# PSUM pools opened from both ends, and one gate's projection moved in among the index scores

## The chip, the core and the metric

The kernel runs on one core of a Trainium2 chip. The metric is the device time of one execution in microseconds (us); lower is better. Five engines matter: TensorE (PE, with its weight loads shown apart as PEld), VectorE (DVE), ScalarE (ACT), GpSimd (POOL) and SyncE (SP), which issues most of the transfers. Each engine works through a list of its own, in order.

## The reference, cut to what matters

The reference is a two-layer encoder on 1024 tokens of width 1024. Layer 0 projects the input once and feeds two groups of heads. Group A is RWKV-7 time mixing (8 heads of 64). Group B is sparse attention: a small indexer scores all admissible keys for each query, the largest 256 scores are kept, and attention runs over these alone. Each group is multiplied by a gate path of its own:

```
score = sum over h of wi[q,h] * relu(qi[q,h] . ki[s])      # the index scores
keep  = the top 256 scores of each query
gate  = silu(x @ W_gate)                                   # 512 columns for A, 512 for B
out   = concat(A * gate_A, B * gate_B) @ W_out
```

Layer 1 is gated linear attention with a gate path and an output projection. After each layer comes h = LayerNorm(alpha * h + sublayer(h)).

## The kernel before

Every projection works on numbers split into a high and a low part, so a product takes three matmuls for each of the eight blocks of the inner dimension. `mm_fm` (L215 to L223) makes 128 output columns for 512 tokens in 24 matmuls, `mm_cols` two such halves for all 1024 tokens, into a two-bank PSUM tile `dn`. `wcols` loads the 128 weight columns (`craw`), casts them to a high part on POOL (`chi`, L231) and makes the low part there (`clo`, in the helper at L103). `craw` has one buffer, `chi` and `clo` have three each.

The stages around the change, in order:

1. The index stage. The loop over `ORD` runs index scores by query tile (0 to 7), queries of the attention (10 and 11), a weight load (9) and keys and values (8). `index_scores` is matmuls L447 into `dn` or `ix`, a relu on ACT (L453) into `rl`, and a multiply-add on DVE (L458) into `sc`.
2. The projection stage, for j from 0 to 3. First comes the rank projection (`rank_inputs`, with a tanh at L686). Then, per j, the three token-shifted projections of group A (`shifted`, with the ACT and DVE steps L549 and L550 into `sh`, which has three buffers), the operands of the recurrence (`operands`, L615 to L634, with POOL multiplies in the helper at L103), and the gates listed in `PG`. `gate(z)` is 48 matmuls, a tanh on ACT (L539), a multiply-add on DVE (L540) and a store `d_gate`. All of this is interleaved with the top-256 selection: counting passes on DVE (L741 to L748) and passes of signs on ACT (L771 to L773), one after the other for each tile.
3. Sparse attention (logits at L925) and RWKV, whose order is pinned; then the output projection of layer 0, layer 1, its gates and its output projection. `gate_piece` (matmuls L243 to L245 into bank `gt`, tanh L1624, multiply-add L1625) is the last gate work; `l1_half` then transposes (L1704) the gated values, casts them (`yh` L1706, `yl` L1707) and multiplies them with the output weights (L868). The last four weight blocks arrive in `wraw` and become `whi` and `wlo` (L182, L183).

A list scheduler fixes each engine's order when the program is built: it takes the instructions in program order as priorities and places each where its plan says its inputs are ready. An engine can't depart from that order on the chip.

PSUM has eight banks. `open_psum` closes the old pool and opens a new one at each stage; a pool is a region, and the first tile of a new pool waits for all of the older pool whose region it takes. The stages use these banks: ps0 (index and projections) `tr` 2, `dn` 2 tiles of two banks, `ix` 2; ps1 (attention and RWKV) `s`, `po`, `g`, `x`, `ca`, `cb`; ps2 `dn`, `tr`; ps3 (layer 1) `att`, `dn`, `tr`, `gt` 2; ps4 (last output projection) `tr` 3, `op` 3.

Of the kernel before, what the change touches and what calls it, by code (L numbers as in the profile page):

```python
# [8 lines left out]
F32 = mybir.dt.float32  # L9
# [4 lines left out]
AF = mybir.ActivationFunctionType  # L14
ALU = mybir.AluOpType
# [3 lines left out]
PSUM = bass.MemoryType.PSUM  # L19
DRAM = bass.MemoryType.DRAM  # L20

P = 128
SEQ = 1024
NT = 8
# [27 lines left out]
SB = 3  # L52
# [15 lines left out]
LG = 7  # L68
QA = (2, 3)
OG = (0, 0, 0, 0, 0, 0, 3, 2, 3, 0, 0)  # L70
ORD = (2, 3, 4, 9, 10, 5, 7, 11, 6, 8)
PG = [[], [0, 1], [], [], [2, 3], [4], [5], [6, 7], [], []]
RK1 = 0

C_R, C_K, C_V, C_WA = 0, 512, 1024, 1536
C_GA, C_QB, C_IX, C_GB = 1664, 2176, 2688, 3112
# [8 lines left out]
def trunk(ctx: ExitStack, tc: tile.TileContext, x, positions, e_w_in, a_mu, a_w0, a_w2, a_a0, a_a2,  # L85
          a_kk_scale, a_ka, a_rk, a_gn_g, a_gn_b, b_kv_norm_g, b_wuk, b_wuv, e_w_out, o_w_in, c_g2,
          c_g_bias, c_norm_g, o_w_out, ln_g, ln_b, out, dbg=None, stop=None):
    nc = tc.nc
    V, A, G, PE = nc.vector, nc.scalar, nc.gpsimd, nc.tensor
# [15 lines left out]
    def gsub(out, a, b):  # L105
        cut(G.tensor_sub, out, a, b)
# [19 lines left out]
    ewi, ewo, owi, owo = e_w_in[0], e_w_out[0], o_w_in[0], o_w_out[0]  # L126
# [10 lines left out]

    psum = {}

    def open_psum(name, dn, **bank):  # L140
        if psum:
            psum["ctx"].close()
        es = ExitStack()
        ctx.callback(es.close)
        psum.update(ctx=es, pool=es.enter_context(tc.tile_pool(name=name, bufs=1, space=PSUM)), dn=dn, bank=bank)

    def dtile():
        return psum["pool"].tile([P, 1024], F32, name="dn", tag="dn", bufs=psum["dn"])

    def ptile(tag, bufs=None):  # L150
        return psum["pool"].tile([P, 512], F32, name=tag, tag=tag, bufs=psum["bank"].get(tag, 1))

    open_psum("ps0", 2, tr=2, ix=2)

    def rsqrt(pool, xin, n, tag):

# [56 lines left out]
    def wblock(wr, w, c0, n, **kw):  # L213
        return [wload(wr, w, c0, n, k, **kw) for k in range(NK)]

    def mm_fm(pst, wb, cs, ah, al, half):

        sl = slice(half * 512, half * 512 + 512)
        for k in range(NK):
            wh, wl = wb[k]  # L220
            PE.matmul(pst, wh[:, cs], ah[:, k, sl], start=(k == 0), stop=False)  # L221
            PE.matmul(pst, wh[:, cs], al[:, k, sl], start=False, stop=False)  # L222
            PE.matmul(pst, wl[:, cs], ah[:, k, sl], start=False, stop=(k == NK - 1))  # L223

    def wcols(pool, w, c0):

        raw = pool.tile([P, NK, P], F32, name="craw", tag="craw", bufs=1)
        nc.sync.dma_start(raw, w[:, c0:c0 + P].rearrange("(k p) c -> p k c", p=P))
        hi = pool.tile([P, NK, P], F32R, name="chi", tag="chi", bufs=3)
        lo = pool.tile([P, NK, P], F32R, name="clo", tag="clo", bufs=3)  # L230
        CPY[0](hi, raw)  # L231
        gsub(lo, raw, f32(hi))
        return [(hi[:, k], lo[:, k]) for k in range(NK)]
# [31 lines left out]
    d_gate = dram.tile([8, P, SEQ], F32, name="d_gate")  # L265
# [6 lines left out]
    def scope():  # L272
        es = ExitStack()
        ctx.callback(es.close)
        return es
# [7 lines left out]
    wr_ctx = scope()  # L283
    wr = wr_ctx.enter_context(tc.tile_pool(name="wr", bufs=1, side="right"))

    xh = big.tile([P, NK, SEQ], F32R, name="xh")
    xl = big.tile([P, NK, SEQ], F32R, name="xl")
# [58 lines left out]
    gt = gt_ctx.enter_context(tc.tile_pool(name="gt", bufs=1))  # L346
# [50 lines left out]
    for t in range(NT):  # L397
        pt = dtile()
# [12 lines left out]
    for t0 in (0, 4):  # L411
        pt = ptile("tr")
# [22 lines left out]
    def index_scores(i):  # L435
        n = P * (i + 1)
        acc = sc[:, soff[i]:soff[i] + n]
        qiT = index_queries(i)
        E = G if i in IXG else V
        for h in range(8):  # L440
            pt = None
            wide = h in IXW
            if wide:
                pt = dtile()
            for a, b in banks(n):
                ps = pt[:, a:b] if wide else ptile("ix")[:, :b - a]
                PE.matmul(ps, qiT[:, h, :], kiT[:, a:b], start=True, stop=True)  # L447
                if wide:
                    if b < n:
                        continue  # L450
                    a, ps = 0, pt[:, :n]
                r = ixp.tile([P, SEQ], F32, name="rl", tag="rl", bufs=2)[:, :b - a]
                A.activation(r, ps, AF.Relu)  # L453
                w = wi_s[:, i, h:h + 1]
                if h == 0:
                    E.tensor_scalar(acc[:, a:b], r, w, None, op0=ALU.mult)
                else:
                    E.scalar_tensor_tensor(acc[:, a:b], r, w, acc[:, a:b], op0=ALU.mult, op1=ALU.add)  # L458
        V.memset(acc[0:CH, n - CH:n], FMIN)

    def keys_values():
        V.tensor_scalar(ssq, ssq, 1.0 / P, RMS_EPS, op0=ALU.mult, op1=ALU.add)
        rs8 = rsqrt(cp, ssq, NT, "rsq8")
        ktm = t1.tile([P, NT, CH], F32, name="ktm")
        for t0 in (0, 4):
            pk = ptile("ix")
            for t in range(t0, t0 + 4):
                cn = t1.tile([P, P], F32, name="cn", tag="cn", bufs=2)
                V.tensor_scalar(cn, ixt[:, t, 0:P], rs8[:, t:t + 1], None, op0=ALU.mult)
                pt = ptile("tr")  # L470
                PE.transpose(pt[:, :P], cn, ident)
                cT = t1.tile([P, P], F32, name="cT", tag="cT", bufs=2)
                A.activation(cT, pt[:, :P], AF.Copy, scale=par[:, KVG:KVG + 1])
                PE.matmul(pk[:, (t - t0) * P:(t - t0 + 1) * P], cT, wkv, start=True, stop=True)
            pk3 = pk.rearrange("p (t q) -> p t q", q=P)
            A.copy(ktm[:, t0:t0 + 4, :], pk3[:, :, 0:CH])
            A.copy(v_tm[:, t0:t0 + 4, :], pk3[:, :, CH:])
        rope(ktm.rearrange("p t (h d) -> p t h d", h=1), NT, 1, 8, 0, 1)
        k4 = [t1.tile([P, SEQ], F32R, name=f"k4{z}", tag="sp4", bufs=2).rearrange("p (t a d) -> p t a d", a=2, d=CH)
              for z in range(2)]  # L480
        kb = ktm[:, :, None, :].to_broadcast([P, NT, 2, CH])
        A.copy(k4[0], kb)
        V.tensor_sub(k4[1], kb, f32(k4[0]))
        for z, dst in ((0, KH2), (1, KL)):
            for t0 in (0, 4):
                pt = ptile("tr")
                for t in range(t0, t0 + 4):
                    PE.transpose(pt[:, (t - t0) * P:(t - t0 + 1) * P], f32(k4[z][:, t].rearrange("p a d -> p (a d)")), ident)
                A.copy(dst[:, t0 * P:(t0 + 4) * P], pt)

    def queries(t0, wb):
# [6 lines left out]
        for t in range(4):  # L498
# [9 lines left out]
                A.copy(qT[:, h0:h0 + 4, :], pt.rearrange("p (h q) -> p h q", q=P))  # L508
            nc.sync.dma_start(d_q[t0 + t], f32(qT))

    for z in ORD:
        if z < NT:
            index_scores(z)
        elif z == 8:
            keys_values()
        elif z == 9:
            wb = wblock(wr, ewi, C_QB, 512)
        else:
            queries(4 * (z - 10), wb)
# [3 lines left out]
    t1_ctx.close()  # L523
    if stop == "idx":
        return
    wr_ctx.close()
    wr_ctx = scope()
    wr = wr_ctx.enter_context(tc.tile_pool(name="wc", bufs=1, side="right"))

    def proj(c0):  # L530
        pt = dtile()
        mm_cols(pt, wcols(wr, ewi, c0), xh, xl)
        return pt

    def gate(z):
        g, j = divmod(z, 4)
        pt = proj((C_GB if g else C_GA) + j * P)
        o = st("sh", bufs=3) if z >= LG else gt.tile([P, SEQ], F32, name="sg")
        A.activation(o, pt, AF.Tanh, scale=0.5)  # L539
        V.scalar_tensor_tensor(o, o, 1.0, pt, op0=ALU.add, op1=ALU.mult)  # L540
        nc.sync.dma_start(d_gate[z], o)
# [157 lines left out]
    for j in range(3):  # L699
        rank_weights(j)  # L700
        for z in PG[2 * j]:
            gate(z)
# [3 lines left out]
        for h in range(2):  # L706
            kk = operands(j, h, r, k, rn, decays(j, h, t2), t2)
            bonus(j, h, v, kk, brk)
            tokens(j, h, v)
        for z in PG[2 * j + 1]:  # L710
            gate(z)
# [101 lines left out]
    for i in SELO:  # L813
        n = P * (i + 1)
        xs = sc[:, rng(i)]
        z = col[i]
# [13 lines left out]
    j = 3  # L830
    rank_weights(j)
    for z in PG[6]:
        gate(z)
# [3 lines left out]
    rn = norms(j, k)  # L837
    for z in PG[8]:
        gate(z)
    dec = [decays(j, 0, t2), decays(j, 1, t3)]  # L840
    for z in PG[9]:
        gate(z)
# [4 lines left out]
    for h in range(2):  # L847
        bonus(j, h, v, kks[h], brk)
    for z in PG[7]:
        gate(z)  # L850
# [35 lines left out]


    inorder = (tc.keep_in_program_order if PIN_ else (lambda ins: ins))
    open_psum("ps1", 0, s=SB)
    at_ctx = scope()  # L890

    qp = ctx.enter_context(tc.tile_pool(name="qp", bufs=1, side="right"))
# [627 lines left out]


    open_psum("ps2", 3, tr=2)
    g_ctx = scope()
    gp = g_ctx.enter_context(tc.tile_pool(name="gp", bufs=1, side="right"))
# [21 lines left out]
    pt = dtile()  # L1546
# [16 lines left out]
    for h in range(4):  # L1563
        pt = dtile()
# [27 lines left out]
    for z, (c0, dst, ex) in enumerate(((O_Q, qg, la), (O_K, kg, eb))):  # L1592
        wb = wpairs(owi, c0)
        for j in range(4):
            pt = dtile()
# [3 lines left out]
    l_ctx.close()  # L1599


    open_psum("ps3", 2, tr=1, gt=2)
    ga_ctx = scope()
    ga = ga_ctx.enter_context(tc.tile_pool(name="ga", bufs=1, side="right"))
    cngh = ga.tile([P, 2], F32, name="cngh")
# [27 lines left out]
    for t in range(NT):  # L1633
# [6 lines left out]
        po = dtile()  # L1640
        for h in range(4):
            o = po[:, h * 256:(h + 1) * 256]
# [106 lines left out]
```

## Time and profile before

| | |
|---|---|
| Median of 3 runs | 1256.58 us (1253.75 to 1260.7) |
| The profiled execution | 1257.07 us, of which the span is 1255.3 us |
| Instructions in the trace | 22100 |
| Granted TensorE clock, mean share of full speed | 0.977 |
| Longest chain: PE, DVE, DMA | 54%, 15%, 9% of the span |

The span runs from the first to the last recorded instruction; the execution's own time is 1.77 us longer. The chain is followed back from the last instruction, at each step to what released it, so its shares say which engine set the end, not which was busy.

### The profile page before, as it was taken

Reading aid. Unit: us, or ns where it says so; the run is one execution under the profiler, and the core shown is the slowest. Engines: PE = TensorE matmul, PEld = TensorE weight load, DVE = VectorE, ACT = ScalarE, POOL = GpSimd, SP = SyncE. Lnnn points to the kernel's source line nnn. Section 1 sums busy time; section 2 is a strip of 40 time slices with the busy share of each in tenths; the row PEclk is TensorE's granted clock in tenths of the full one; section 3 lists DMA queues with packets and bytes.
Section 4 is the critical chain, followed back from the end, with each engine's and each line's share of the span. In section 5 each row is a group of like instructions: output and inputs, shape, how many; then the busy total and the mean of one; then the engine's idle time right before and its main releaser. Section 6 shows DMA issues by size and latency. Waiting matters only on the chain.

```text
span 1255.3 us, 22100 instructions
## 1 busy us (share of the span) xinstructions
PE 1165.0 (93%) x8125; PEld 934.3 (74%) x8125; DVE 764.7 (61%) x1795; ACT 640.5 (51%) x1395; POOL 409.2 (33%) x723
## 2 busy tenths in 40 slices
PE   7998799989999877989888999999999999998997
PEld 6986587767677666777776777787788788886885
DVE  5145869999985866687776544982601134534666
ACT  5247859889878465666675321324811034413010
POOL 3233853545453034355454300603033120221000
PEclk9999899999999978999998999999999999999999
DMA  6102312544434584444454555842022010014221
GB/s 217 39 5 84 101 51 60 155 101 136 120 101 118 170 222 126 118 117 111 115 148 119 149 169 186 271 159 74 1 68 67 7 62 1 29 40 143 76 101 51
DMA packets 166095, 131.40 MB, mean 105 GB/s; under 512 B 61684, under 2 KB 139556, under 8 KB 165988
## 3 DMA queue, kind: packets, MB, share of 16 engines
q1 hardware_dynamic: 162864, 122.46, 33.5%
q10 hardware_dynamic: 3124, 7.54, 1.9%
q8 instruction: 64, 1.05, 0.3%
q14 instruction: 43, 0.35, 0.1%
HBM read 86.44 MB, written 42.99 MB: 103 GB/s over the span
## 4 chain that ended last, share of the span: by engine, by line
PE 54%; DVE 15%; DMA 9%; issue 8%; ACT 7%; POOL 4%; SPq 2%; DVEq 0%; ACTq 0%; POOLq 0%
PE op L868 7%; PE s L868 5%; DVE fe L741 4%; PE dn L221 4%; PE dn L222 4%; PE dn L223 4%; PE gt L245 2%; PE gt L244 2%; PE gt L243 2%; DMA wraw<-in_e_w_in_dram 2%; PE s L954 1%; PE tr L244 1%; PE tr L243 1%; PE tr L245 1%; PE po L988 1%
## 5 line engine op out<-in xcount | busy, mean ns | idle before, releaser
L103 POOL TENSOR_TENSOR w<-qT,w 128x256 fp32r<-128x256 f32 x104 | 77.7, 782 | 208.0 <-ACT w L203 198.8
L221 PE MATMUL dn<-xh,chi 128*128 128x512 f32 x336 | 135.3, 403 | 5.5 <-DVE sh L550 4.9
L223 PE MATMUL dn<-xh,clo 128*128 128x512 f32 x336 | 133.9, 399 | 0.0
L222 PE MATMUL dn<-xl,chi 128*128 128x512 f32 x336 | 133.3, 397 | 0.0
L203 ACT CAST w<-qT 128x512 fp32r<-128x512 f32 x64 | 38.9, 620 | 105.2 <-PE dn L223 68.1
L741 DVE TENSOR_SCALAR_CACHE_REDUCE fe<-sc,F 128x512 bf16<-128x512 f32 (+2 forms) x93 | 81.6, 877 | 2.5
L221 PEld LDWEIGHTS dn<-xh,chi 128*128 128x128 f32 x336 | 64.0, 190 | 23.1 <-DVE sh L550 6.6
L222 PEld LDWEIGHTS dn<-xl,chi 128*128 128x128 f32 x336 | 63.9, 190 | 15.8 <-issue 2.9
L223 PEld LDWEIGHTS dn<-xh,clo 128*128 128x128 f32 x336 | 63.8, 190 | 14.0 <-issue 1.0
L103 POOL TENSOR_TENSOR clo<-craw,chi 128x256 fp32r<-128x256 f32 x84 | 69.9, 862 | 0.8
L868 PE MATMUL op<-w,yh 128*128 128x512 f32 x192 | 60.4, 399 | 1.7 <-ACT yh L1706 1.7
L458 DVE SCALAR_TENSOR_TENSOR sc<-rl,wi_s,sc 128x384 f32<-128x384 f32 (+5 forms) x42 | 45.1, 1075 | 23.7 <-ACT rl L453 21.2
L935 ACT ACTIVATE w<-w,am 128x128 f32<-128x128 f32 (+7 forms) x64 | 49.6, 775 | 18.8 <-DVE am L933 17.7
L954 PE MATMUL s<-ident,w 128*128 128x128 f32 x288 | 48.9, 296 | 8.9 <-ACT w L935 4.0
L927 DVE CUSTOM_DVE_ANT_0 w<-s,bias_s 128x512 f32<-128x512 f32 (+1 forms) x80 | 45.3, 592 | 18.5 <-PE s L926 18.1
L103 POOL TENSOR_TENSOR vg<-vg,sg 128x256 f32<-128x256 f32 x32 | 24.1, 775 | 99.5 <-DVE vg L1671 53.7
L956 ACT COPY pT<-s 128x512 f32<-128x512 f32 x72 | 42.0, 585 | 20.0 <-PE s L954 19.1
L243 PE MATMUL gt<-w,hh 128*128 128x512 f32 x128 | 51.9, 406 | 0.0
L245 PE MATMUL gt<-w,hl 128*128 128x512 f32 x128 | 51.2, 400 | 0.0
L244 PE MATMUL gt<-w,hh 128*128 128x512 f32 x128 | 51.1, 399 | 0.0
L221 PE MATMUL dn<-hh,w 128*128 128x512 f32 x128 | 50.6, 395 | 0.0
L222 PE MATMUL dn<-hl,w 128*128 128x512 f32 x128 | 50.6, 395 | 0.0
(478 smaller groups left out, 3327.7 us busy)
## 6 DMA issues: line engine op xcount, KB each, us to landing
qT<-in_o_w_in_dram SPq DMA_DIRECT2D x48, 256.0 KB
craw<-in_e_w_in_dram SPq DMA_DIRECT2D x21, 512.0 KB
xt<-in_x_dram SPq DMA_DIRECT2D x8, 512.0 KB
d_q<-qiT SPq DMA_DIRECT2D x8, 512.0 KB
d_ar<-ar SPq DMA_DIRECT2D x8, 512.0 KB
AT<-d_ar SPq DMA_DIRECT2D x32, 128.0 KB
BK<-d_bk SPq DMA_DIRECT2D x8, 512.0 KB
BD<-d_bd SPq DMA_DIRECT2D x8, 512.0 KB
```

The source lines that it names most:

```text
L103: return [f(out[:, a:min(n, a + w)], *(z[:, a:min(n, a + w)] for z in ins)) for a in range(0, n, w)]
L221: PE.matmul(pst, wh[:, cs], ah[:, k, sl], start=(k == 0), stop=False)
L222: PE.matmul(pst, wh[:, cs], al[:, k, sl], start=False, stop=False)
L223: PE.matmul(pst, wl[:, cs], ah[:, k, sl], start=False, stop=(k == NK - 1))
L243: PE.matmul(pst, ah[:, k, sl], wh, start=(k == 0), stop=False)
L244: PE.matmul(pst, ah[:, k, sl], wl, start=False, stop=False)
L245: PE.matmul(pst, al[:, k, sl], wh, start=False, stop=(k == NK - 1))
L741: V.tensor_scalar(junk[:, :P * (i + 1)], sc[:, rng(i)], Ff[:, z] if b < 31 else 0.0, None, op0=ALU.is_ge, op1=ALU.add, accum_out=cnt[:, z])
L868: ins = PE.matmul(pt, a[:, k, :], b, start=(k == 0 and z == 0), stop=(k == NK - 1 and z == 2))
L927: V.tensor_tensor_reduce(ps[h][:, a:b], pt, bias[:, a:b], 1.0, -3e38, op0=ALU.add, op1=ALU.max, accum_out=mx[:, h, z:z + 1])
L935: A.activation(ps[k][:, :n], ps[k][:, :n], AF.Exp, scale=0.125, bias=m[:, k:k + 1], accum_out=rsum[:, k:k + 1])
L954: inorder(PE.transpose(pt[:, j * P:(j + 1) * P], OUT[i]["ps"][2 * j + s][:, kt * P:(kt + 1) * P], ident))
```

## The change

`open_psum` may now open two pools: the tags named in `other` get a pool that is laid out from the other end of PSUM. ps0 puts `tr` and `ix` there, ps1 `s` and `po`, ps3 `gt`; ps2 and ps4 stay single. Each of the two pools is a region of its own, so a tile of the next stage waits for the one it takes.

Gate 0 is taken out of the projection stage (`PG[1]` loses it) and put into the `ORD` loop between the index scores of tile 7 with the queries of the upper half, and those of tile 6. It is done by `gate_halves`: the same weights and the same 48 matmuls, but in two halves of one `ix` bank each, with a tanh and a multiply-add of 512 columns for each half in place of one of 1024. The pool of projection weights (`wc`) is opened there (step 12) and no longer after the loop.

```
-ORD = (2, 3, 4, 9, 10, 5, 7, 11, 6, 8)
-PG = [[], [0, 1], [], [], [2, 3], [4], [5], [6, 7], [], []]
+ORD = (2, 3, 4, 9, 10, 5, 7, 11, 12, 20, 6, 8)
+PG = [[], [1], [], [], [2, 3], [4], [5], [6, 7], [], []]
...
-    def open_psum(name, dn, **bank):
+    def open_psum(name, dn, other=(), **bank):
...
+        pool = es.enter_context(tc.tile_pool(name=name, bufs=1, space=PSUM))
+        high = es.enter_context(tc.tile_pool(name=name + "h", bufs=1, space=PSUM, side="right")) if other else pool
+        psum.update(ctx=es, pool=pool, high=high, other=other, dn=dn, bank=bank)
...
-        return psum["pool"].tile([P, 512], F32, name=tag, tag=tag, bufs=psum["bank"].get(tag, 1))
+        return psum["high" if tag in psum["other"] else "pool"].tile([P, 512], F32, name=tag, tag=tag, bufs=psum["bank"].get(tag, 1))
...
-    open_psum("ps0", 2, tr=2, ix=2)
+    open_psum("ps0", 2, ("tr", "ix"), tr=2, ix=2)
...
+    def gate_halves(z):
+        g, j = divmod(z, 4)
+        wb_ = wcols(wr, ewi, (C_GB if g else C_GA) + j * P)
+        o = gt.tile([P, SEQ], F32, name="sg")
+        for half in range(2):
+            pt, oh = ptile("ix"), o[:, half * 512:half * 512 + 512]
+            mm_fm(pt, wb_, slice(0, P), xh, xl, half)
+            A.activation(oh, pt, AF.Tanh, scale=0.5)
+            V.scalar_tensor_tensor(oh, oh, 1.0, pt, op0=ALU.add, op1=ALU.mult)
+        nc.sync.dma_start(d_gate[z], o)
+
     for z in ORD:
-        if z < NT:
+        if z >= 20:
+            gate_halves(z - 20)
+        elif z == 12:
+            wr_ctx.close()
+            wr_ctx = scope()
+            wr = wr_ctx.enter_context(tc.tile_pool(name="wc", bufs=1, side="right"))
+        elif z < NT:
...
-    wr_ctx.close()
-    wr_ctx = scope()
-    wr = wr_ctx.enter_context(tc.tile_pool(name="wc", bufs=1, side="right"))
...
-    open_psum("ps1", 0, s=SB)
+    open_psum("ps1", 0, ("s", "po"), s=SB)
...
-    open_psum("ps3", 2, tr=1, gt=2)
+    open_psum("ps3", 2, ("gt",), tr=1, gt=2)
```

## Rows read from the trace of the kernel before

**Rows 1.** Page, part 1: busy us, share of span, instructions.

```profile
PE 1165.0 (93%) x8125; PEld 934.3 (74%) x8125; DVE 764.7 (61%) x1795; ACT 640.5 (51%) x1395; POOL 409.2 (33%) x723
```

**Rows 2.** Busy time by stretch: index, then projections.

```profile
core 0: us, PE busy (x) PEld busy (x) DVE busy (x) ACT busy (x) POOL busy (x), PEclk, DMA share, GB/s
131.00:156.47 25.47, 17.80 (x83) 11.90 (x81) 21.98 (x23) 21.42 (x36) 21.08 (x17) 0.92 0.38 125
...
156.00:252.00 96.00, 95.53 (x420) 76.63 (x421) 83.26 (x179) 78.25 (x175) 46.92 (x60) 1.00 0.31 87
252.00:258.00 6.00, 2.10 (x7) 0.82 (x6) 5.96 (x10) 5.18 (x11) 3.36 (x3) 1.00 0.89 219
172.00:398.00 226.00, 218.41 (x907) 168.79 (x905) 195.97 (x393) 201.03 (x483) 108.10 (x136) 0.98 0.42 115
```

**Rows 3.** Timeline of POOL, 118 to 150: start, us, what, idle before.

```profile
129.56 5.68 POOL L103 TENSOR_TENSOR clo<-craw,chi 128x256 fp32r<-128x256 f32 x4
...
144.22 4.75 POOL L103 TENSOR_TENSOR clo<-craw,chi 128x256 fp32r<-128x256 f32 x4
```

**Rows 4.** Timeline of PE at 156 and DVE at 172.

```profile
156.47 0.50 PE L221 MATMUL dn<-xh,chi 128*128 128x512 f32 x1 [0.54 <-ACT rl L453]
...
171.78 0.17 DVE L555 MEMSET bones<- 128x128 f32 x1 [7.77 <-PE tr L488]
```

**Rows 5.** Timeline of ACT, 177 to 180.

```profile
177.48 1.28 ACT L686 ACT_TABLE_LOAD   x1
178.77 1.06 ACT L686 ACTIVATE sh<-sh 64x1024 f32<-64x1024 f32 x1
```

**Rows 6.** Timeline of ACT and DVE at 221: gate 0 as it ran.

```profile
221.31 1.01 ACT L539 ACTIVATE sg<-dn 128x1024 f32<-128x1024 f32 x1
...
222.89 1.22 DVE L540 SCALAR_TENSOR_TENSOR sg<-sg,dn 128x1024 f32<-128x1024 f32 x1
```

**Rows 7.** Timeline of all engines, 251 to 258.

```profile
251.48 2.84 POOL L103 TENSOR_TENSOR kk<-sh 128x256 f32<-128x256 f32 x2 [2.33 <-DVE tha L624]
...
252.30 0.39 PE L223 MATMUL dn<-xh,clo 128*128 128x512 f32 x1
...
254.35 1.11 ACT L549 ACTIVATE sh<-dn,drv 128x1024 f32<-128x1024 f32 x1 [0.54 <-POOL kk L103]
...
257.71 0.50 PE L221 MATMUL dn<-xh,chi 128*128 128x512 f32 x1 [2.21 <-DVE sh L550]
```

**Rows 8.** Timeline of all engines, 436 to 439.

```profile
436.42 0.69 DVE L642 TENSOR_TENSOR kk<-ix,sh 128x512 f32<-128x512 f32 x1
...
437.36 1.15 DVE L540 SCALAR_TENSOR_TENSOR sh<-sh,dn 128x1024 f32<-128x1024 f32 x1
...
438.56 0.33 PE L925 MATMUL s<-KH,qT 128*128 128x128 f32 x1 [3.91 <-DVE sh L540]
```

**Rows 9.** Timeline of all engines, 1143 to 1152: last gate to output projection.

```profile
1143.80 0.72 ACT L206 ACTIVATE w<-qT,cngh 128x512 fp32r<-128x512 f32 x1 [3.20 <-DMA qT<-in_o_w_out_dram]
...
1144.43 0.58 ACT L1624 ACTIVATE sg<-gt 128x512 f32<-128x512 f32 x1
...
1145.22 0.68 DVE L1625 SCALAR_TENSOR_TENSOR sg<-sg,gt 128x512 f32<-128x512 f32 x1
...
1145.96 2.82 PE L1704 MATMUL tr<-ident,vg 128*128 128x128 f32 x12 [3.31 <-DVE sg L1625]
...
1149.04 0.72 ACT L182 ACTIVATE whi<-wraw,cngh 128x512 fp32r<-128x512 f32 x1 [0.59 <-DMA wraw<-in_o_w_out_dram]
...
1149.67 1.54 ACT L1706 CAST yh<-tr 128x512 fp32r<-128x512 f32 x3
...
1150.29 0.73 PE L868 MATMUL op<-w,yh 128*128 128x512 f32 x2 [1.51 <-ACT yh L1706]
```

**Rows 10.** Timeline of DVE and PE, 1165 to 1175.

```profile
1165.47 0.73 DVE L183 SCALAR_TENSOR_TENSOR wlo<-wraw,cngh,whi 128x512 fp32r<-128x512 f32 x1
...
1173.64 1.47 PE L1704 MATMUL tr<-ident,vg 128*128 128x128 f32 x12
```

More of the change, by code (lines that the diff above doesn't have):

```diff
@@ L144, in open_psum @@
         ctx.callback(es.close)
-        psum.update(ctx=es, pool=es.enter_context(tc.tile_pool(name=name, bufs=1, space=PSUM)), dn=dn, bank=bank)
+        pool = es.enter_context(tc.tile_pool(name=name, bufs=1, space=PSUM))
+        high = es.enter_context(tc.tile_pool(name=name + "h", bufs=1, space=PSUM, side="right")) if other else pool
+        psum.update(ctx=es, pool=pool, high=high, other=other, dn=dn, bank=bank)
     def dtile():
```

## The prediction

> **What bounds the kernel now.** I read the page's first part, then the busy times by stretch, then the timeline wherever the diff touches something. The first part makes TensorE look like the bound: 93% of the span, with weight loads at 74% and nothing else above 61% [rows 1]. That average hides stages with different limits, so I read each stage that the change touches.
>
> In the index stage from 131.00 to 156.47 PE works 17.80 us of 25.47 and is idle for 7.67. DVE is idle for 3.49, ACT for 4.05, POOL for 4.39 [rows 2]: nobody is full, the engines take turns. In the projections after it PE looks saturated, 95.53 of 96.00 us up to 252. Then, from 252 to 258, it works 2.10 us of 6.00 while DVE works 5.96 [rows 2]. That hole is the key row of this case. Between the last two gates the product r1 ends its matmuls with the one at 252.30, and the next product starts only at 257.71, released by DVE's L550 [rows 7]. L550 needs L549 on ACT, which at 254.35 was released by POOL's kk, which itself had waited for DVE [rows 7]. So the chain of j=0's operands on DVE, ACT and POOL ends last there, and PE had run ahead of it as far as the three `sh` buffers let it.
>
> **Gate 0 moved: what the index stage pays.** A projection is 48 matmuls; at 95.53 us for 420 instructions one is 0.2275 us [rows 2], so 10.9 us of PE. Its weights' low part is made on POOL at 129.56 to 135.24, in quarters, so the matmuls can begin near 131 [rows 3]. This is the slot of the first weights, which the rank projection uses now; that gets the second, ready at 148.97, and still in time for a start at 156.47 [rows 3, 4]. With PE's 7.67 idle us as cover, 10.9 − 7.67 = 3.2 spill over. Some of PE's 17.80 busy us ran at a granted clock of 0.92 [rows 2]; at full clock they would be 0.08 × 17.80 = 1.4 less, and a spill of 1.8. I take the middle, +2.5.
>
> ACT gets two tanh of 0.58 and the table load of 1.28, DVE two multiply-adds of 0.68 [rows 5, 9]. That is 2.44 and 1.36 against idle times of 4.05 and 3.49 [rows 2]: the idle time hides them; without it they would add their 3.8. So the bounds are 0 (PE's idle fits it and more) and 10.9 + 3.8 = 14.7 (no cover at all). The spill reaches the next stage, because the rank projection starts as PE comes free [rows 4], and DVE's first step of the selection's stage waited 7.77 us for PE [rows 4]. The store of the gate, 128 × 1024 words or 0.52 MB, is now issued by SP in this stretch, where DMA moves 125 GB/s [rows 2]: 4 us of transfer, ahead of SP's later weight loads. Those weights have 156.47 − 148.97 = 7.5 us of slack, so nothing; uncovered it is within the bound above. What POOL does for gate 0 is in the first weights that it prepares now anyway.
>
> **Gate 0 moved: what the projections get back.** PE loses 10.9 us before 252. But PE already waits there for the chain of j=0, so that work is cover for a wait: the hole of about 5 us grows to about 15, and PE's saving is nothing by itself. What the chain itself loses counts: on DVE the multiply-add of 1.22 at 222.89 [rows 6], DVE working 83.26 of 96.00 us there [rows 2]; I take 1.0. On ACT the table load at 177.48, 1.28, and the tanh of 1.01 [rows 5, 6]; ACT works 89% of 172 to 398 (201.03 of 226) and its sign passes follow each other, so part of 2.29: 0.6. Bounds for both together: 0, and the full 10.9 of PE if PE is the limit after all.
>
> The Trainium skill, Perfetto Trace Analysis, section Identifying the Most-Contended Engine, says that matmul busy time is a poor measure of TensorE's headroom because matmuls are pipelined. It wants the share of weight loads instead, and calls the engine of highest occupancy the contended one. In 172 to 398 that is ACT with 89% against 75% of weight loads (168.79 of 226), though the matmuls show 97% [rows 2]. By it, removing matmuls gives nothing here; by the matmul row alone it would give 10.9. The hole at 252 agrees with the page.
>
> The Trainium skill, ScalarE: Activation LUTs, section What ACT_TABLE_LOAD costs, adds a drain of about 1380 ns to each load. The trace does not show one: the ACTIVATE at 178.77 follows the load's 1.28 at once [rows 5]. By the page the index stage would pay 1.4 more and the sum below would be −2.5.
>
> **PSUM of attention.** The first logits at 438.56 waited 3.91 us for DVE's L540, the last gate's reader of `dn` [rows 8]. In the new layout `s` takes the end where `tr` and `ix` were, whose last reader L642 is done at 437.11 [rows 8]. PE could start up to 1.4 earlier, but the attention's first DVE steps still stand behind L540 until 438.51. I take −0.5, between 0 and −1.4. From ps1 to ps2 and ps2 to ps3 nothing changes, as ps2 is one pool over all banks and each of its neighbours waits for all of it.
>
> **PSUM of the last projection.** Here PE stands still. The last gate matmul ends at 1145.96 − 3.31 = 1142.65, and the transposes wait for L1625 on DVE, behind a tanh that sat on ACT behind a weight cast waiting 3.20 us for its transfer [rows 9]. Then the first product waits 1.51 us for `yh` [rows 9]. After the change the transposes' banks were freed long before, by `att`, `dn` and `tr`; only `gt` is read late. They can run at 1142.65, or among the gates. PE's idle there is 3.31 + 1.51 = 4.82, and the twelve transposes took 2.82 us after the stall against 1.47 without one [rows 9, 10]: at most −6.2. The casts stay behind the tanh (ending 1145.01) and two weight casts of 0.72; so the first is done near 1146, and 1150.29 − 1146.0 = −4.3. Lower end: zero, if ACT's order keeps `yh` behind `whi`, which waits for its transfer until 1149.04 [rows 9]; that transfer's buffer is freed by the last gate matmul, which doesn't move. The rest of the weights would not stop it: the last low part is done at 1166.20, and the products that need it run until 1173.64 [rows 10].
>
> **Sum.** +2.5 − 1.0 − 0.6 − 0.5 − 4.3 = −3.9. Against the profiled execution, 1257.07 − 3.9 = 1253.2; that execution is 0.5 above the median of the runs. I predict 1253.0.
>
> **Rivals.**
> - *PE is the bound after all.* The 10.9 us come through, as the new plan lets the matmuls of j=1 and j=2 move up. For it: 97% busy in 172 to 398. Against it: the hole at 252, and a selection that needs no matmul. It replaces −1.6 by −10.9: 2.5 − 10.9 − 0.5 − 4.3 = −13.2, about 1244.
> - *The halves block the index scores* (ends slower). In PE's fixed order 24 matmuls in a row, 5.5 us, stand ahead of the matmuls of tile 6, which ACT and DVE need; they run dry, and the idle is spent waiting for weights instead. Place: 131 to 160. The stage pays 10.9: −3.9 + 8.4 = +4.5, about 1261.6, and up to 1265.4 at 14.7. It decides from a delay of 6.4, where the other terms are used up. For it: PE's waits in this stage are short turns. Against it: nothing makes tile 6 wait except order.
> - *Nothing at the last projection.* ACT's order keeps `yh` behind `whi`. Then the sum is +0.4, about 1257.5. For it: the 1149.04 row. Against it: in a plan, a cast whose input is ready goes ahead of one with a transfer still out.
>
> **How the numbers follow.** Forecast 0.42 (its own range 1249 to 1257), PE the bound 0.28, nothing at the last projection 0.18, index blocked 0.12. What a measurement of this kernel can tell from no change is about 0.5%, 6.3 us: faster is below 1250.3, slower above 1262.9. Faster takes nearly all of the PE rival (0.26) and a tenth from the forecast's low end: 0.36. Slower takes half of the blocked index stage and what its upper end shares with the third rival: 0.09. The rest, 0.55, is the same. The range runs from 1243.5, just below the PE rival, to 1261.6, the blocked stage's own figure; outside lie half of the blocked cases (0.06) and deeper versions of the PE rival (0.1).
>
> **What would show it.** Right: PE busy for nearly all of 131 to 156; a table load there and not at 177; the rank projection starting near 159; a hole in PE of some 15 us where 5 were, before the second product of j=1; the first logits released by L642; the transposes L1704 without a wait for L1625, and the first product near 1146. Wrong: no hole before the product after r1, with the end of the selection some 8 us earlier; a rank projection that starts after 163; or `yh` still behind `whi`.

## The result, and the profile after

The change makes the kernel slower: 1265.61 us median of 19 runs (1260.17 to 1276.83) against 1258.51 of 19 runs before. The ratio is 1.0056, with an interval of 1.0040 to 1.0073. The forecast was 1253.0, and the range ended at 1261.6.

The profiled execution of the change took 1260.9 us, 3.8 more than that of before. Its busy times by stretch, first the index stage as in [rows 2], then the part of it in which most of the gate's matmuls stand, the first products after it, the hole in PE, and the projections:

```profile
core 0: us, PE busy (x) PEld busy (x) DVE busy (x) ACT busy (x) POOL busy (x), PEclk, DMA share, GB/s
131.00:156.47 25.47, 21.81 (x110) 16.87 (x110) 18.16 (x19) 19.15 (x31) 20.45 (x20) 1.00 0.43 145
131.62:147.07 15.45, 15.45 (x76) 12.41 (x76) 9.22 (x9) 11.46 (x16) 12.77 (x13) 1.00 0.38 136
156.00:172.00 16.00, 13.55 (x42) 9.42 (x41) 13.93 (x18) 8.25 (x14) 5.35 (x6) 0.68 0.24 67
252.00:266.00 14.00, 2.21 (x3) 0.67 (x4) 13.82 (x27) 10.36 (x21) 10.66 (x11) 0.61 0.37 105
172.00:398.00 226.00, 209.65 (x880) 162.65 (x879) 194.82 (x391) 193.38 (x463) 109.97 (x131) 0.96 0.38 104
```

In 131.00 to 156.47 PE was busy 4.0 us more (21.81 for 17.80), and from 131.62 to 147.07 without a gap. DVE was busy 3.8 us less (18.16 for 21.98): the scores were pushed out, into 156 to 172. Before, the scores of tile 7 ran from 131.89 to 147.07, and the same columns read for that stretch:

```profile
131.89:147.07 15.18, 9.77 (x45) 6.49 (x44) 11.98 (x9) 12.18 (x18) 15.18 (x12) 0.89 0.46 154
```

There PE was idle for 5.41 us, and POOL for none. PE's and DVE's timelines of the change show how the scores were pushed out (its lines are 3 higher than before for the scores, 16 higher from the projections on):

```profile
131.62 0.50 PE L226 MATMUL ix<-xh,clo 128*128 128x512 f32 x1 [1.03 <-POOL clo L103]
...
134.48 0.63 PE L450 MATMUL dn<-kiT,qiT 128*128 128x512 f32 x2
...
163.82 0.79 PE L224 MATMUL dn<-xh,chi 128*128 128x512 f32 x1 [0.79 <-ACT rl L456]
```

```profile
136.21 1.28 DVE L461 SCALAR_TENSOR_TENSOR sc<-rl,wi_s,sc 128x1024 f32<-128x1024 f32 x1 [2.67 <-ACT rl L456]
...
139.20 1.81 DVE L461 SCALAR_TENSOR_TENSOR sc<-rl,wi_s,sc 128x1024 f32<-128x1024 f32 x1 [1.71 <-ACT rl L456]
...
180.17 0.17 DVE L571 MEMSET bones<- 128x128 f32 x1 [9.83 <-PE tr L491]
```

Between 131.62 and 134.48 twelve gate matmuls run in a row, and only then the score pair of a head of tile 7. The program puts the gate behind tile 7; it is the scheduler's order that has 44 of the 48 matmuls among that tile's scores. ACT's relu and DVE's multiply-add of that head wait, DVE for 2.67 us, and for 1.71 at the next. The rank projection starts at 163.82 where it started at 156.47 [rows 4], and bones comes at 180.17 for 171.78.

At the two ends of the projections, and at the last transition:

```profile
260.97 2.08 PE L656 MATMUL ix<-kk,brk 128*128 128x512 f32 x2 [9.01 <-POOL kk L103]
265.86 0.77 PE L224 MATMUL dn<-xh,chi 128*128 128x512 f32 x1 [2.82 <-DVE sh L566]
```

```profile
1148.16 0.82 PE L1720 MATMUL tr<-ident,vg 128*128 128x128 f32 x6
...
1149.56 0.72 ACT L209 ACTIVATE w<-qT,cngh 128x512 fp32r<-128x512 f32 x1 [3.28 <-DMA qT<-in_o_w_out_dram]
...
1152.14 0.57 ACT L1722 CAST yh<-tr 128x512 fp32r<-128x512 f32 x1
...
1152.76 1.17 PE L884 MATMUL op<-w,yh 128*128 128x512 f32 x2 [3.78 <-ACT yh L1722]
```

The hole in PE has grown, as forecast, though less: to 9.01 + 2.82 = 11.8 us of idle time. Before, it was 2.21 at the product [rows 7] and 1.69 at L640, which is L656 here, so 3.9 in all; the forecast had 5 and 15. The transposes L1720 (L1704 before) no longer wait for the gate [rows 9]; the first product now waits for the cast `yh` instead, 3.78 us.

So that runs can be compared, I read six stretches from each kernel's profiled execution: tile 7 and tile 6 (between the memsets that end a tile's scores; before, these are at 131.89, 147.07 and 161.48), the time from the first score multiply-add (72.2 before) to bones and to RWKV's first instruction (443.74 before), from there to the last gate's tanh (middle), and from that tanh to the last multiply-add with the output product (last). All are us; the ratio is to before, with its interval.

| kernel | tile 7 | tile 6 | bones | RWKV | middle | last | ratio |
|---|---|---|---|---|---|---|---|
| before | 15.2 | 14.4 | 99.6 | 371.5 | 700.7 | 102.0 | |
| the change | 22.6 | 15.1 | 107.5 | 377.9 | 699.6 | 100.0 | 1.0056 (1.0040 to 1.0073) |
| e1 | 15.9 | 13.9 | 100.2 | 374.1 | 705.4 | 101.0 | 1.0005 (0.9981 to 1.0028) |
| e2 | 22.4 | 15.1 | 106.9 | 379.6 | 711.2 | 102.5 | 1.0167 (1.0144 to 1.0190) |
| e3 | 15.2 | 15.8 | 105.5 | 376.9 | 704.5 | 99.9 | 1.0062 (1.0041 to 1.0082) |
| e4 | 15.2 | 14.4 | 99.7 | 377.0 | 700.3 | 102.8 | 1.0011 (0.9985 to 1.0037) |
| e5 | 15.9 | 13.9 | 99.9 | 371.7 | 713.9 | 101.3 | 1.0096 (1.0071 to 1.0120) |
| e6 | 22.3 | 15.1 | 107.1 | 379.7 | 702.8 | 100.6 | 1.0058 (1.0039 to 1.0077) |
| e7 | 15.2 | 14.4 | 93.2 | 367.6 | 716.6 | 102.8 | 1.0089 (1.0070 to 1.0108) |
| e8 | 15.2 | 14.4 | 93.3 | 366.3 | 701.9 | 101.3 | 0.9972 (0.9954 to 0.9991) |
| e9 | 18.3 | 15.5 | 113.5 | 384.8 | 711.4 | 100.3 | 1.0143 (1.0114 to 1.0173) |
| e10 | 15.9 | 13.9 | 93.4 | 367.2 | 703.3 | 101.4 | 0.9979 (0.9958 to 1.0001) |
| e11 | 22.5 | 15.1 | 101.9 | 376.1 | 706.9 | 100.3 | 1.0063 (1.0041 to 1.0085) |
| e12 | 18.5 | 14.7 | 102.1 | 385.2 | 710.8 | 100.4 | 1.0168 (1.0139 to 1.0196) |
| e13 | 18.2 | 17.9 | 105.7 | 376.8 | 701.0 | 101.6 | 1.0043 (1.0017 to 1.0069) |
| e14 | 15.2 | 14.5 | 99.7 | 379.4 | 717.1 | 100.6 | 1.0189 (1.0154 to 1.0224) |

Each stretch is from one execution; where the order of the instructions is the same, tile 7 differs by up to 0.7 us between kernels. Two readings hold over the whole table: "last" is 99.9 to 101.6 with two pools in ps3 and 102.0 to 102.8 with one (before, e2, e4, e7), and "middle" varies by 17 us, though apart from the pools no kernel changes anything in it.

### The profile page after: what moved, and what is told of

Same layout as the page of the kernel before. It is cut to its first block, busy times and chain, and to the rows that moved or that the text cites. A ratio compares the mean times of both kernels' runs of the same rounds, so it can differ in the third digit from the quotient of the medians.

```text
span 1259.2 us, 22105 instructions
## 1 busy us (share of the span) xinstructions
PE 1166.8 (93%) x8125; PEld 935.2 (74%) x8125; DVE 766.0 (61%) x1796; ACT 641.3 (51%) x1396; POOL 409.6 (33%) x723
## 4 chain that ended last, share of the span: by engine, by line
PE 53%; DVE 16%; issue 8%; DMA 8%; ACT 8%; POOL 5%; SPq 1%; DVEq 0%; POOLq 0%; ACTq 0%
PE op L884 7%; PE dn L224 4%; PE dn L225 4%; PE dn L226 4%; PE s L884 3%; DVE fe L757 3%; PE gt L248 2%; PE gt L247 2%; PE gt L246 2%; DMA wraw<-in_e_w_in_dram 1%; PE s L970 1%; ACT fs L787 1%; PE tr L246 1%; PE tr L247 1%; PE tr L248 1%
## 5 line engine op out<-in xcount | busy, mean ns | idle before, releaser
L224 PE MATMUL dn<-xh,chi 128*128 128x512 f32 x320 | 129.9, 406 | 5.1 <-DVE sh L566 4.3
L226 PE MATMUL dn<-xh,clo 128*128 128x512 f32 x320 | 129.0, 403 | 0.0
L225 PE MATMUL dn<-xl,chi 128*128 128x512 f32 x320 | 128.7, 402 | 0.0
L103 POOL TENSOR_TENSOR clo<-craw,chi 128x256 fp32r<-128x256 f32 x84 | 73.2, 900 | 1.0
L951 ACT ACTIVATE w<-w,am 128x128 f32<-128x128 f32 (+7 forms) x64 | 49.5, 774 | 14.5 <-DVE am L949 14.2
L103 POOL TENSOR_TENSOR vg<-vg,sg 128x256 f32<-128x256 f32 x32 | 24.1, 774 | 100.3 <-DVE vg L1687 64.5
L234 POOL CAST chi<-craw 128x1024 fp32r<-128x1024 f32 x21 | 22.2, 1055 | 90.2 <-PE dn L225 56.5
```

Source lines behind the costliest of these rows:

```text
L103: return [f(out[:, a:min(n, a + w)], *(z[:, a:min(n, a + w)] for z in ins)) for a in range(0, n, w)]
L951: A.activation(ps[k][:, :n], ps[k][:, :n], AF.Exp, scale=0.125, bias=m[:, k:k + 1], accum_out=rsum[:, k:k + 1])
```

## The experiments

Theory Q puts the loss in PE's queue in the index stage: the gate's matmuls stand ahead of the score matmuls there, and the delay goes on to the end. Its rivals are the new layout (L), the gate's weights on POOL (W), and the gate's work on ACT and DVE (A). Theories C and B concern what sets the end behind that stage.

**e1: the pools alone.** The two-part `open_psum`, with `ORD` and `PG` of before.

> The PSUM pools in two parts, gate 0 left at j=0. Theory Q (PE's queue: the loss is made in the index stage, where the gate's matmuls stand ahead of tile 7's score matmuls, and the pools only help): the index and projection stages as before, rank projection at 156.5, DVE's bones at 171.8; the first output product some 3 us sooner after the last gate matmul; ratio to before 0.997 to 0.999. Rival L (the layout: the tiles tr and ix at the other end delay the index stage or the attention): bones later than 173 or the total slower than before, ratio 1.002 or more.

Ratio 1.0005 (0.9981 to 1.0028), bones at 172.4. The layout delays nothing in the index stage, so rival L is out there. RWKV starts 2.6 us later than before, and 1.3 sooner in e8 than in e7, which differ in the layout too; so what the layout does in between is not settled. The first output product comes 6.0 us after the last gate matmul instead of 7.6, so 1.6 sooner and not 3, and the gain of 1 us in "last" is below what the timing resolves.

**e2: the gate alone.**

```diff
-    open_psum("ps0", 2, ("tr", "ix"), tr=2, ix=2)
+    open_psum("ps0", 2, (), tr=2, ix=2)
```

and the same in ps1 and ps3.

> Gate 0 moved as in the change, every PSUM stage in one pool as before. Theory Q: bones near 180, 8 us late, and nothing won at the last projection, so slower than the change itself: ratio to before 1.006 to 1.009. Rival L: bones near 172 and a ratio within 0.998 to 1.002.

Bones 7.3 us later than before, measured from the first score: theory Q. The total, 1.0167, is worse than either theory said. The rest is in "middle", 10.5 us longer, where SP's weight loads of layer 1 stand in another order; whether that is the cause was not tested.

**e3: gate 0 behind all index scores.**

```diff
-ORD = (2, 3, 4, 9, 10, 5, 7, 11, 12, 20, 6, 8)
+ORD = (2, 3, 4, 9, 10, 5, 7, 11, 6, 8, 12, 20)
```

> The change, with gate 0 put behind the index scores of tile 6 and keys and values in the loop. Theory Q: what costs is any place where the gate's matmuls come before score matmuls in PE's order. If the plan still fills them in among the scores, bones is near 180 again; if it puts them behind, the rank projection starts 10.9 us late and bones comes near 183. Either way slower than before, ratio 1.003 to 1.009. Rival W (gate's weights: POOL makes them ahead of tile 6's qs, and that is what is late): with the weights prepared last, tile 6's scores are on time and bones is at 172 to 175.

Tile 7 is back at 15.2, but bones is still 5.9 us late. Gate 0's matmuls now stand in PE's queue between the scores and the sixteen key transposes for which bones waits. So the cost is not special to the scores: it is paid wherever gate work stands ahead of what the selection needs.

**e4: no gate 0 at all.** In the kernel before, `gate(0)` only stores `d_gate[0]`, from other data.

> The kernel before without gate 0 at all: its matmuls, tanh, multiply-add and weights are left out, d_gate[0] is stored from other data, and the gated output of one block is therefore another. What the projection stage gives back when gate 0 leaves it. By the prediction's term -1.6 us (chain of DVE and ACT, PE's matmuls are cover): hole of PE near 252 of about 12 to 15 us, end of the selection 1 to 2 us sooner, ratio 0.998 to 1.000. By the rival that PE is the bound: -10.9 us, ratio 0.991.

Ratio 1.0011: taking 10.9 us of matmuls out of j=0 gives nothing. The hole's row shows where they went:

```profile
255.53 2.08 PE L643 MATMUL ix<-kk,brk 128*128 128x512 f32 x2 [12.40 <-DVE ld L603]
```

PE waits 12.40 us there instead of 1.69: before, gate 0 had filled a wait. RWKV even starts 5.5 us later here, behind a wait of PE at the first logits (7.0 us) for which the profile shows no releaser; "last" and "middle" are as before.

**e5: six matmuls instead of 48.**

```diff
-            mm_fm(pt, wb_, slice(0, P), xh, xl, half)
+            mm_fm(pt, wb_, slice(0, P), xh, xl, half, 1)
```

where the last argument limits the blocks of the inner dimension to one.

> The change, with 3 of the 24 matmuls in each half of gate 0 (one block of the inner dimension out of eight, so the gate is another); its weights on POOL, both tanh, the table load, both multiply-adds and the store stay. Theory Q (PE's queue: what costs is the 10.9 us of matmuls ahead of tile 7's score matmuls): PE gets 1.4 us, and bones falls from 180.2 to 172 to 174. Rivals A (ACT and DVE: tanh, table load and multiply-add are what delays) and W (POOL makes gate 0's weights and waits for the next ones ahead of the queries' split): bones stays at 177 or later.

Tile 7 takes 15.9 and bones is 0.3 us late, with the weights, both tanh, the table load, the multiply-adds and the store in place. Rival A is out as the cause in the change. Rival W is out for tile 7 alone: for tile 6, POOL splits the queries (`qs`) at 142.52 here, ahead of the low part of the next weights (`clo`, 144.88), as before, while in the change their order is the other way round (see e13). Its total of 1.0096 is again a longer "middle" (713.9) and says nothing of the index stage.

**e6: 48 matmuls without tanh and multiply-add.**

> The change with all 48 matmuls of gate 0 in the index stage, but without its tanh and multiply-adds (so the table load goes back to the rank projection's tanh, and d_gate[0] is stored from other data). Theory Q: bones at 178 to 180, nearly all of the delay stays. Rival A: bones at 172 to 174.

Tile 7 takes 22.3, bones is 7.5 us late, ratio 1.0058: the change's loss with none of its work on ACT and DVE.

**e7 and e8: the opposite shift.** The key transposes are held ahead of all but the first 24 matmuls of the rank projection. e7 is the kernel before with this, e8 has the two pools too.

```diff
+            if k == 0 and "T" in HOLD and HOLD["n"] > 0:
+                after(HOLD["T"], ins)
...
+                    HOLD["T"] = PE.transpose(...)
```

> The kernel before, with the order of PE held so that the sixteen key transposes, for which the selection's first DVE step waits, come behind the first 24 matmuls of the rank projection instead of behind 38 and 69. Theory C (the time from bones to the second product of j=1, 86 us, and from there to RWKV, 186 us, is a chain of DVE and ACT and then of PE, so a shift of bones passes to the end one to one, either way): bones at 166, 5 to 6 us early, hole's end near 252, total -5 to -6, ratio 0.995 to 0.997. Rival F (the delay of bones is made up or lost for other reasons, PE's work sets the end): bones early, the end within 2 us of before, ratio 0.998 to 1.001.

> The same order of PE with the change's PSUM pools in two parts and gate 0 left at j=0. Theory C and a gain of 1 to 2 us at the last projection: total -6 to -8, ratio 0.994 to 0.996. Rival F: ratio 0.998 to 1.001.

In e8 the transposes follow each other, and DVE waits 1.31 us for them instead of 7.77 (before, the two eights stood behind 38 and 58 matmuls; the expectation has 69 for the second):

```profile
163.91 1.09 PE L497 MATMUL tr<-ident,k 128*128 128x128 f32 x8 [0.54 <-ACT k L491]
165.34 1.06 PE L497 MATMUL tr<-ident,k 128*128 128x128 f32 x8 [0.33 <-ACT KH L498]
```

```profile
166.50 0.17 DVE L564 MEMSET bones<- 128x128 f32 x1 [1.31 <-PE tr L497]
```

Bones is 6.3 us sooner and RWKV 5.2 us (3.9 in e7). But the shift did not arrive by the path of theory C. The hole's end did not move (258.15 in e8, 257.71 before). Nor is it the selection that RWKV waits for: in the kernel before, its last step on DVE (L824) starts at 414.41, and the first logits only at 438.56 [rows 8]. Counted from the first score, that step comes in e8 11.6 us sooner, the last matmul of the projections 2.1 and the first logits 6.2. In e3, e11 and e14 that step comes 2.7 to 4.6 us sooner than before, and yet RWKV starts 4.6 to 7.9 us later, behind projections that end 7.3 to 11.2 later. RWKV starts 6.0 to 10.3 us after the last projection matmul in every kernel (14.4 in e4), so its start follows the end of the projections; what links that to bones stays open. e8 is the only kernel whose interval lies below 1: 0.9972 (0.9954 to 0.9991). e7, with the same order there, is at 1.0089, by a "middle" of 716.6.

**e9: the gate's matmuls spread.** Three matmuls behind each score pair, the first half in tile 7, the second in tile 6.

```diff
+            after(SM[(7, 6)[half]][k], PE.matmul(pt, wh, xh[:, k, sl], start=(k == 0), stop=False))
```

> The change with gate 0's 48 matmuls held behind single score pairs: the three of block k behind the pair of head k, of tile 7 for the first half and of tile 6 for the second. Theory Q, in its exact form (a batch of 9 to 12 gate matmuls ahead of a score pair holds that head back; three at a time fit PE's waits): bones at 173 to 176 instead of 180.2, total 3 to 6 us below the change, ratio to before 1.000 to 1.003. If it is the 10.9 us of PE and not their batching: bones stays at 179 to 181, ratio 1.005 or more.

The theory in its exact form fell. Tile 7 takes 18.3 with 24 matmuls in threes, and 18.2 in e13 with 24 in batches: within a tile the amount counts, and not the batches. But the other 24 cost tile 6 only 1.1 us (0.3 in e12). From the first score multiply-add to the last it takes 91.9 us here, 95.3 in the change and 87.9 before, so with the matmuls in both tiles the scores lose 3.9 us (3.2 in e12) and not 7.3. Whether that is a gain is not settled, as the new order also put 10 of the 24 PE instructions of keys and values behind the first projection matmuls. Bones and the total can't tell: the key transposes stand behind 69 projection matmuls, and bones is 13.9 us late.

**e10, e11 and e12: combinations.** e10 is e8 without gate 0, e11 the change with the early transposes, e12 that with the spread matmuls.

> Two pools, the early key transposes, and gate 0 left out (d_gate[0] from other data, so one gated block is another). With the early transposes alone bones moved by 6 us and the second product of j=1 not at all (258.15 against 257.71). Theory B (two limits lie within some 5 us of each other there: the chain of DVE and ACT from bones, and PE's queue): without gate 0 the second product of j=1 comes at 251 to 254, and the total falls by 3 to 6 us against the early transposes alone, ratio to before 0.992 to 0.995. Rival: PE's 10.9 us count in neither kernel; the second product stays near 258, ratio 0.996 to 0.998.

> The change with the early key transposes: both limits eased, the chain by 6 us of the 8 that it lost. Bones at 174 to 175, the second product of j=1 at 260 to 261, total 4 to 6 us below the change, ratio to before 1.000 to 1.003.

> The change with its gate matmuls spread and the early key transposes. By theories Q and B together bones is at 168 to 171 and PE has 10.9 us less before the hole, so the second product of j=1 comes at 254 to 257, ratio to before 0.993 to 0.998. If the early transposes alone are all that counts: 0.997.

e10, at 0.9979, is no faster than e8: even with the chain 6 us ahead, PE's 10.9 us count for nothing in the total, and theory B fell there. The second product of j=1 comes at 255.28, between what the two sides expected. e11 regains 5.6 us at bones and 1.8 at RWKV, and its ratio of 1.0063 is that of the change, so the 4 to 6 us that were expected of it did not come. In e12 bones comes at 176.7 instead of 168 to 171, 2.6 us later than before, and RWKV is 13.7 us late; its order of the projections is another one, and the cause was not sought.

**e13: half of the matmuls.** As e5, with four blocks of eight.

> The change with 12 of the 24 matmuls in each half of gate 0 (four blocks of the inner dimension, so the gate is another). The time from the first score multiply-add to the last was 87.9 us before, 95.3 in the change, 88.2 with 3 matmuls in each half. If the loss goes with PE's time (theory Q by amount), half of 7.4: 91 to 92.5, bones 3 to 4.5 us late. If a threshold decides (below PE's idle 7.67 nothing, above it the rest): 5.5 us of matmuls fit, 88 to 89, bones within 1 us of before.

Tile 7 takes 18.2, halfway: by amount, and no threshold. But tile 6 takes 17.9, so the scores take 94.5 us instead of 91 to 92.5, and bones is 6.1 us late instead of 3 to 4.5: half of the matmuls still cost most of the delay. POOL's timeline shows a second price:

```profile
141.25 6.71 POOL L103 TENSOR_TENSOR clo<-craw,chi 128x256 fp32r<-128x256 f32 x4
147.93 3.37 POOL L103 TENSOR_TENSOR qs<-ixt,qs 128x256 fp32r<-128x256 f32 x2
```

```profile
149.69 0.91 PE L429 MATMUL tr<-ident,qs 128*128 128x128 f32 x4 [3.25 <-POOL qs L103]
```

The split of tile 6's queries (`qs`) stands behind the low part of the next weights (`clo`); before, `qs` came at 141.86 and `clo` at 144.22 [rows 3]. The change has the reversed order too, with `clo` at 142.26:

```profile
147.02 2.39 POOL L103 TENSOR_TENSOR qs<-ixt,qs 128x256 fp32r<-128x256 f32 x2
```

```profile
147.80 0.66 PE L429 MATMUL tr<-ident,qs 128*128 128x128 f32 x4 [0.73 <-POOL qs L103]
```

There PE, busy without a gap until 147.07, waits 0.73 us for the first half and 0.54 for the second. So POOL's order and PE's matmuls are two limits that end within 1.3 us of each other in the change. The chain that the profile follows back from the end even runs through POOL there (`clo` at 142.31, `qs` at 147.06), and not through the gate's matmuls. Rival W is therefore not out for tile 6. No run has the 48 matmuls in batches with `qs` ahead of `clo`, so what they would cost without POOL's order was not measured.

**e14: all of the change but the place.** Two halves in `ix` banks, the weight pool opened in the loop, but at j=0.

> Two pools, the weight pool opened in the loop, gate 0 in two halves in the ix banks, but at its old place at j=0: all of the change but the place. If the place is the cause: scores 88 us from first to last, bones at 172 to 173, ratio to before 0.998 to 1.003. If the halves, their banks or the early weight pool cost: ratio 1.004 or more, and the stage that lengthens shows which.

Scores 15.2 and 14.5, bones where it was: neither the halves nor the weight pool cost anything in the index stage. The total of 1.0189 is made elsewhere: PE waits 14.7 us in one piece for POOL's `kk` in the projections, and "middle" is 16.4 us longer. As a test of the total it is inconclusive.

## Why the prediction was wrong, point by point

**The step that failed** is "With PE's 7.67 idle us as cover, 3.2 spill over … I take the middle, +2.5". It measured +7.9 at bones (107.5 less 99.6). The 7.67 us were not the cover. They are PE's idle time over two tiles, and 44 of the 48 matmuls went into the first, tile 7. There PE was idle for 5.41 us, in waits for other engines: 2.81 of them were two waits for POOL's `qs` (1.80 and 1.01, before the transposes L507 at 136.95 and 138.62), and POOL was busy for all of that stretch. "Nobody is full" was an average too. In the change PE is full there, the score pairs come when the queue lets them, and tile 7 takes 7.4 us longer, so about 3.5 of the 10.9 us found cover. The runs give the price in tile 7 by dose: 6 matmuls +0.7 (within the scatter), 24 matmuls (5.5 us) +3.0 to 3.1, 48 (10.9 us) +7.1 to 7.4, so 0.55 to 0.7 us for each us of PE. In tile 6 it was less (e9), and POOL's order sets a second limit close behind the first (e13). ACT and DVE add nothing (e6), and the forecast's hiding of their 2.44 and 1.36 us was right (e5). The forecast's own sign of being wrong, "a rank projection that starts after 163", came: 163.82.

**The rival was there** and had the right mechanism in the main: "the halves block the index scores". It was put at tile 6, while the matmuls went into tile 7; its price of 10.9 was 3 too high; and with 0.12 it got too little chance. "Nothing makes tile 6 wait except order" was offered against it, but order is enough. The range ended at that rival's middle figure, so even the right mechanism left the median 4 us outside.

**The delay goes on to the end,** as forecast, in this one profile: of +7.9 at bones, +6.4 are left at RWKV. The giving back was forecast as −1.0 − 0.6 − 0.5 = −2.1 and came to −1.5. That it is the same delay is not shown: in e4 and e14 bones is within 0.1 us of before, and RWKV starts 5.5 and 7.9 us later. That PE's matmuls at j=0 are cover is shown by e4 and e10. The Trainium skill, Perfetto Trace Analysis, section Identifying the Most-Contended Engine, had pointed the same way, and these two runs agree with it: PE's matmuls were busy 97% of that stretch, and removing 10.9 us of them gave 1.0011 in e4.

**Attention's PSUM:** the first logits wait for L658 (the old L642) and no longer for the last gate, as forecast. What it brings RWKV can't be told from the rest of the −1.5.

**The last projection** was mis-sized: −4.3 forecast, −2.0 measured in "last". Part of that lay in the forecast's own sum: a tanh that ends at 1145.01, two weight casts of 0.72 and the cast `yh` itself, 0.57, end near 1147 and not 1146. The transposes run at once, but the wait moved to `yh`, which stands on ACT behind a weight cast that waits 3.28 us for its transfer. The first product came 4.4 us after the last gate matmul (1148.32 to 1152.76) instead of 7.6, so 3.2 sooner and not 4.3; and 1.2 of that are lost again, as the first six products take 3.2 us and not 2.0, behind the casts that follow.

**The table load** moved to the first tanh of gate 0, and no drain is seen there either:

```profile
139.18 1.28 ACT L521 ACT_TABLE_LOAD   x1
140.48 0.60 ACT L521 ACTIVATE sg<-ix 128x512 f32<-128x512 f32 x1
```

The ACTIVATE follows 0.02 us after the load's end, and the relu ahead of the load ended at 139.17. The drain of about 1380 ns that the Trainium skill, ScalarE: Activation LUTs, section What ACT_TABLE_LOAD costs, adds to a load does not appear in this trace.

**The sum of the profiled executions** closes: a start 0.5 later, +6.4 at RWKV, −1.1 in "middle", −2.0 in "last" make +3.8, and 1260.9 − 1257.07 is 3.8. **What stays open** is the median: it moved by 7.1. The profiled execution of the change lies 4.7 below its median, that of before 1.4 below its own, so 3.3 us of the loss are in executions that no profile shows. Nor is it settled what makes "middle" vary from 700 to 717 when an earlier stage is planned anew.

## What to carry to other kernels

Idle time of an engine inside a loop that passes from engine to engine is poor room for other work: in tile 7 each us of matmuls put there cost 0.55 to 0.7 us. Read such idle time over the very stretch in which the work will stand, and look at every engine there: over two tiles PE had 7.67 us and nobody was full, in tile 7 alone PE had 5.41 and POOL none. When work is moved, look also at what the scheduler turns round on the other engines, as POOL's `qs` and `clo` here. Before moving work out of a stretch, ask whether it fills a wait: gate 0 did, and removing it gave nothing (1.0011). Look instead for what a chain waits for in another engine's queue: sixteen transposes put ahead of projection matmuls brought, with the two pools, 0.28%, where the pools alone brought nothing that can be measured. Without the pools the same order came out at 1.0089, so compare stage by stage: a new plan can cost more elsewhere than the change gains.

## What the hardware showed that was not expected

After a stretch in which PE was busy for 11.64 of 16.80 us (147.00 to 163.80), the rank projection ran slowly: the matmuls from 164.41 to 169.53 start 0.43 us apart, those from 170.13 on 0.23, and the granted clock of 156 to 172 is 0.68 of full speed, a mixture of its two levels (1.2 and 2.4 GHz), against 1.00 before [rows 2]. The key transposes stand behind 30 matmuls of it instead of 38, and still come about 1 us later after its start: 173.58 − 163.82 = 9.8 against 165.22 − 156.47 = 8.8. What made the clock fall was not tested.
